# A hybrid attention and expert-lookup layer on one core: the order around the head groups' norms and the way of the gate row

## The chip, the core and the metric

The kernel runs on one core of a Trainium2 chip (trn2). The metric is the device time of one execution in microseconds, lower is better; several runs are given by their median. The engines are named as in the profile: PE (TensorE), PEld (its weight loads), DVE (VectorE), ACT (ScalarE), POOL (GpSimd) and SP (SyncE), which issues the kernel's DMAs in one queue, in order.

## The reference, cut to what matters

One decoder layer for 256 tokens of width 2048, in float32. `c` is a condition vector that makes six rows of scales, shifts and gates.

```python
mod = jnp.dot(jax.nn.silu(c), w_ada) + b_ada
sh1, sc1, g1, sh2, sc2, g2 = split(mod, 6)
h = layer_norm(x) * (1 + sc1) + sh1
proj = jnp.dot(h, w_in)                       # 4160 columns
qa, ka, va, cq, ckv, kr = split(proj)         # va: columns 2048 to 3071
o_a = dilated_mixture(rope(qa), rope(ka), va)           # 8 heads of 128
o_b = mla_attention(... rms_norm(cq), rms_norm(ckv) ...)  # 8 heads of 128
o = concatenate([rms_norm(o_a, g_out_a), rms_norm(o_b, g_out_b)])
mix = jnp.dot(o, w_o)
x = layer_norm(alpha * x + g1 * mix, ln1_g, ln1_b)
h = layer_norm(x) * (1 + sc2) + sh2
x = layer_norm(alpha * x + g2 * peer(h, ...), ln2_g, ln2_b)
```

Both groups' outputs are normed over all 1024 columns of the group (root of the mean square), so a group's norm needs its last head.

## The kernel before, in words

**Layout.** Tokens lie on the 128 partitions in two halves (`th`), features along the free axis. A weight comes from memory in pieces of 512 rows by 512 columns, 1 MB each, loaded by SP into a ring of three `raw` buffers. A product with nearly full float32 precision takes three passes (`mm3`, L139 to 142): ACT casts the piece to `hi` (L101), DVE subtracts for `lo` (L103), two halves to a piece, in rings of four halves each; PE then multiplies hi·hi, hi·lo and lo·hi. Some early pieces are multiplied as plain float32 (L334).

**The condition rows.** `w_ada` has 96 blocks of 1 MB. `ada` (L207 to 213) loads one into a buffer (a ring of two, tag "ada") and DVE multiplies and sums it against the activated condition in two passes (L212). The first 32 blocks are woven into w_in by hand (`ada_in`). The other 48 of sub-layer 1 and 2 come from a generator, `ada_rest` (L246): `ada_pull(n)` draws the next n, first the 16 of the gate row G1, then the second sub-layer's shifts and scales. Where it is called, and with which number, is in the tuples `PULLS`, `PULL_WO` and `PULL_PQ` (L42 on).

**w_in** (L315 to 346): four groups of 512 input rows (kg), eight pieces of 512 columns in each, in two halves of the rows. Sums over the groups are added in `proj` in SBUF by DVE (L346). Group 3 is ordered by the attention: `latents` (L519) takes pieces 6 and 7 (the latents of group B), then 0, 2, 4; then 1, 3 and 5 (L580). Piece 4 has the values of dilated heads 0 to 3, piece 5 those of heads 4 to 7.

**Attention.** Heads run one after another: `attend` (L415) has PE compute scores, DVE add the mask and take the maximum, ACT the exponential, PE three transposes (L438), ACT a copy, PE the product with the values (L442 to 444), ACT the scaled result into `proj` (L446, helper L240). Group A has the dilated heads, group B the latent ones. The order is a0, a1, a2, a3, then b0 to b3, then b4 to b7, each followed by a pull, then the norm of group B, a4 and a5, group B's operands, a6 and a7.

**Norms and operands.** `row_norm` (L458) has ACT square all 1024 columns with a running sum (L462), DVE and ACT make the inverse root (`rstd_of`, L166: a square root on ACT and six small DVE operations), and the rows are scaled in place, one half by DVE (L468), the other by ACT. `to_operand` (L488) then transposes 512 columns at a time on PE (L481), scales them on ACT with the gain (L485), casts (L160) and subtracts (L161) into the operand `act` of w_o.

**w_o** (L239 on): 16 pieces. Steps 0 to 3 use the rows of group B only (column blocks 0 and 1); they are put ahead of the norm of group A in the text (L624). Then `g1b`, the gate row on all partitions, is made by `spread_cols` (L230): for each of 16 columns a diagonal tile on DVE (L235) and a product with ones on PE (L236), four copies on ACT (L237). Steps 4 to 11 follow; at the end of a column block `residual` (L642) multiplies with `g1b`, adds x and takes statistics; the first is at step 7. The layer norm, w_pq and the expert stages follow; they fill three quarters of the span.

**What sets the order.** Each engine runs its instructions in a fixed order, made when the program is built: the text's order is the priority, and an operation that a model of the engines has ready comes ahead of one that waits. `issue_after` puts the instructions of a block behind a given one on its engine.

## Time and profile before

| | |
|---|---|
| median of 3 runs | 2043.37 us (2042.28 to 2044.26) |
| the profiled execution's own time | 2044.22 us |
| its span | 2042.4 us |
| mean granted clock of PE | 0.984 |
| busy share PE, DVE, ACT, POOL | 97%, 73%, 51%, 0% |
| moved by DMA | 554.82 MB |

Times in the trace count from the start of the span. A line of the windows view has the stretch, its length, then for PE, PEld, DVE, ACT and POOL the busy time with the number of instructions in brackets, then the granted clock of PE as a share of full speed (1.00 is 2.4 GHz, 0.50 is 1.2 GHz), the share of the DMA engines' time, and GB/s. A line of the timeline has start, duration, engine, line of the kernel, operation, output and inputs, shapes, count, and in square brackets how long the engine was idle before and what released it. Product durations include the array's depth; from start to start they are shorter.

### The profile page before, as it was taken

To read this page: it belongs to the slowest core of one execution; us is meant where nothing else is said; L and a number is where in the kernel's file an instruction comes from. 1 tells how busy PE (TensorE), PEld (TensorE's weight loads), DVE (VectorE), ACT (ScalarE), POOL (GpSimd) and SP (SyncE) were. 2 spreads that over 40 slices of the span, in tenths; PEclk is the share of its full clock that TensorE was granted. 3 is DMA by queue.
4 is the path that set the end of the run, shared out by engine and by line. 5 is a ranking of instruction groups with operands and counts; after the bars stand their busy time and mean duration, and the time that the engine had idled before them with its cause. 6 is when DMAs were issued, how large, how long until landed. Compare 5 with 4: busy or idle time off the path is not lost.

```text
span 2042.4 us, 26235 instructions
## 1 busy us (share of the span) xinstructions
PE 1973.8 (97%) x10072; PEld 1644.3 (81%) x10072; DVE 1497.3 (73%) x2344; ACT 1048.2 (51%) x1538; POOL 0.2 (0%) x4
## 2 busy tenths in 40 slices
PE   6999998988999999999999999999999999999997
PEld 4567686778998888888888888888888788888886
DVE  7588987889799868677777766686776666554557
ACT  2333457435444665677777775444444444444451
POOL 0000000000000000000000000000000000000000
PEclk7999998998999999999999999999999999999999
DMA  8887887867646566667777668989999988765552
GB/s 349 338 332 304 314 324 268 331 267 277 241 147 215 219 239 254 235 255 273 270 287 265 266 238 308 316 337 324 329 337 324 304 290 286 278 227 202 189 207 102
DMA packets 142830, 554.82 MB, mean 272 GB/s; under 512 B 10864, under 2 KB 77552, under 8 KB 84848
## 3 DMA queue, kind: packets, MB, share of 16 engines
q1 hardware_dynamic: 142704, 553.14, 73.5%
q8 instruction: 79, 1.29, 0.2%
q14 instruction: 47, 0.39, 0.1%
HBM read 502.76 MB, written 50.34 MB: 271 GB/s over the span
## 4 chain that ended last, share of the span: by engine, by line
PE 85%; DVE 9%; DMA 3%; ACT 2%; issue 1%; SPq 0%; DVEq 0%; ACTq 0%
PE u_ps L135 21%; PE u_ps L136 11%; PE v_ps L141 10%; PE v_ps L140 10%; PE v_ps L142 10%; PE win_ps L334 3%; DVE ada L212 2%; PE win_ps L141 2%; DMA gl<-g_d 2%; PE win_ps L142 2%; PE g_ps L942 2%; PE win_ps L140 1%; PE wo_ps L142 1%; PE wo_ps L141 1%; PE wo_ps L140 1%
## 5 line engine op out<-in xcount | busy, mean ns | idle before, releaser
L135 PE MATMUL u_ps<-act,hi_u 128*128 128x512 f32 x2048 | 721.6, 396 | 0.0
L136 PE MATMUL u_ps<-act,lo_u 128*128 128x256 f32 x2048 | 575.1, 281 | 0.9 <-DVE lo_u L103 0.9
L135 PEld LDWEIGHTS u_ps<-act,hi_u 128*128 128x128 f32 x2048 | 384.5, 188 | 87.7
L101 ACT CAST hi_v<-raw_v 128x1024 fp32r<-128x1024 f32 x244 | 256.8, 1054 | 332.0 <-PE v_ps L142 298.6
L103 DVE TENSOR_TENSOR lo_v<-raw_v,hi_v 128x1024 fp32r<-128x1024 f32 x244 | 295.6, 1222 | 173.0 <-ACT hi_v L101 172.9
L103 DVE TENSOR_TENSOR lo_u<-raw_u,hi_u 128x1024 fp32r<-128x1024 f32 x256 | 312.3, 1221 | 137.7 <-ACT hi_u L101 136.5
L136 PEld LDWEIGHTS u_ps<-act,lo_u 128*128 128x128 f32 x2048 | 386.6, 189 | 3.9 <-DVE lo_u L103 3.7
L141 PE MATMUL v_ps<-lo_v,whi 128*128 128x512 f32 x976 | 380.0, 389 | 2.3 <-DVE lo_v L103 2.3
L140 PE MATMUL v_ps<-hi_v,whi 128*128 128x512 f32 x976 | 379.9, 389 | 1.0 <-DVE W L798 1.0
L142 PE MATMUL v_ps<-hi_v,wlo 128*128 128x512 f32 x976 | 379.7, 389 | 0.0
L101 ACT CAST hi_u<-raw_u 128x1024 fp32r<-128x1024 f32 x256 | 267.3, 1048 | 174.4 <-PE u_ps L135 163.3
L141 PEld LDWEIGHTS v_ps<-lo_v,whi 128*128 128x128 f32 x976 | 183.2, 188 | 41.0 <-DVE lo_v L103 3.5
L140 PEld LDWEIGHTS v_ps<-hi_v,whi 128*128 128x128 f32 x976 | 183.2, 188 | 40.1 <-DVE W L798 1.8
L142 PEld LDWEIGHTS v_ps<-hi_v,wlo 128*128 128x128 f32 x976 | 183.2, 188 | 38.1
L212 DVE SCALAR_TENSOR_TENSOR ada<-ada,cb 128x1024 f32<-128x1024 f32 x160 | 191.0, 1218 | 9.9 <-DMA ada<-in_w_ada_dram 9.8
L937 DVE TENSOR_TENSOR o<-eq,gT 128x1024 fp32r<-128x1024 f32 x64 | 78.3, 1223 | 33.3 <-PE g_ps L942 33.3
L334 PE MATMUL win_ps<-raw_win,hmod 128*128 128x512 f32 x192 | 86.4, 605 | 1.2 <-ACT hmod L305 1.2
L799 ACT ACTIVATE W<-W 128x512 f32<-128x512 f32 x64 | 40.7, 636 | 73.4 <-DVE W L798 73.4
L140 PE MATMUL wpq_ps<-act,hi_wpq 128*128 128x256 f32 x256 | 73.6, 290 | 2.3 <-ACT act L160 2.1
L142 PE MATMUL wpq_ps<-act,lo_wpq 128*128 128x256 f32 x256 | 72.8, 286 | 0.5 <-DVE lo_wpq L103 0.5
L141 PE MATMUL wpq_ps<-act,hi_wpq 128*128 128x256 f32 x256 | 73.0, 286 | 0.0
L101 ACT CAST hi_win<-raw_win 128x1024 fp32r<-128x1024 f32 x40 | 40.9, 1049 | 61.4 <-PE win_ps L142 30.8
(329 smaller groups left out, 2407.1 us busy)
## 6 DMA issues: line engine op xcount, KB each, us to landing
raw_u<-in_u_dram SPq DMA_DIRECT2D x128, 1024.0 KB, 5.3
raw_v<-in_v_dram SPq DMA_DIRECT2D x122, 1024.0 KB, 6.6
ada<-in_w_ada_dram SPq DMA_DIRECT2D x80, 1024.0 KB, 6.9
raw_win<-in_w_in_dram SPq DMA_DIRECT2D x32, 1024.0 KB, 8.9
g_d<-stg SPq DMA_DIRECT2D x16, 2048.0 KB, 7.2
gl<-g_d SPq DMA_DIRECT2D x32, 1024.0 KB, 10.1
raw_wo<-in_w_o_dram SPq DMA_DIRECT2D x16, 1024.0 KB, 6.9
raw_wpq<-in_w_pq_dram SPq DMA_DIRECT2D x16, 1024.0 KB, 6.9
```

The costliest lines, as they stand in the source:

```text
L101: nc.scalar.copy(hi, raw[:, 2 * j:2 * j + 2, :])
L103: nc.vector.tensor_sub(lo, raw[:, 2 * j:2 * j + 2, :], hi.bitcast(F32))
L135: nc.tensor.matmul(pss[e], hi[:, i, es], act[:, k], start=first and j == 0 and i == 0, stop=False)
L136: nc.tensor.matmul(pss[e][:, 1], lo[:, i, es], act_hi[:, k, :], start=False, stop=last and j == 1 and i == 3)
L140: nc.tensor.matmul(o, sh, mh, start=start, stop=False)
L141: nc.tensor.matmul(o, sh, ml, start=False, stop=False)
L142: nc.tensor.matmul(o, sl, mh, start=False, stop=stop)
L212: nc.vector.scalar_tensor_tensor(w[:, z, :], w[:, z, :], 1.0, cb[:, z * 1024:(z + 1) * 1024], op0=ALU.mult, op1=ALU.mult, accum_out=(modc, ...
L334: nc.tensor.matmul(ps[th], act[:, i, ts], src[:, i, :], start=i == 0, stop=i == 3)
L799: nc.scalar.activation(ws, ws, AF.Gelu)
L937: nc.vector.tensor_mul(o2, eq.unsqueeze(2).broadcast_to(both), gT[:, four, :].bitcast(F32).unsqueeze(3).broadcast_to(both))
L942: nc.tensor.matmul(ps[:, q * T:(q + 1) * T], o1[:, 2 * j + q, :], o2[:, 2 * j + q].rearrange("p z n -> p (z n)"), start=True, stop=True)
```

## The change

- Piece 5 of w_in's group 3 (the values of a4 to a7) leaves its place between the latents and a0. It is loaded and split ahead of head b7, and its products are issued behind b7's last product, in front of the norm of group B. The scores of a4 and a5 come in front of it.
- Each group's squares are split: those of the first seven heads are taken early (`early_squares`), only the last head's at the end. The inverse root takes fewer DVE operations.
- The norm and the operands of group A come ahead of w_o's steps 0 to 3 in the text. The pulls of these steps are put behind that norm on DVE.
- The gate row is transposed as soon as its sixteen blocks are there, written to memory (`row_d`), and read back to all partitions by one DMA, in place of the spread.
- Pulls move: six into w_in's group 1 (one behind each of the six sets of pieces), none any more with piece 5 or behind b4 to b6 and b7, and other numbers in w_o.

```diff
-PULLS = (2, 1, 1, 3, 0, 1, 1, 1, 3, 1, 0, 1)
-PULL_WO = (2, 3, 0, 1, 1, 1, 1, 1, 0, 0, 1, 2)
+PULL_IN = (0, 1, 0)
+PULLS = (2, 1, 1, 3, 0, 1, 1, 1, 3, 1, 0, 0)
+PULL_WO = (0, 1, 1, 1, 1, 1, 1, 1, 1, 1, 1, 2)
...
     def rstd_of(pool, var, n, eps):
         uid[0] += 1
         ve = pool.tile([P, n], F32, tag=f"rs_ve{n}", name=f"rs_ve{uid[0]}", bufs=1)
         nc.vector.tensor_scalar(ve, var, eps, None, op0=ALU.add)
+        return rstd_from(pool, ve, n)
+
+    def rstd_from(pool, ve, n):
         r = pool.tile([P, n], F32, tag=f"rs_r{n}", name=f"rs_r{uid[0]}", bufs=4)
         nc.scalar.activation(r, ve, AF.Sqrt)
         nc.vector.reciprocal(r, r)
         t = pool.tile([P, n], F32, tag=f"rs_t{n}", name=f"rs_t{uid[0]}", bufs=1)
         nc.vector.tensor_mul(t, r, r)
-        nc.vector.tensor_mul(t, t, ve)
-        nc.vector.tensor_scalar(t, t, -0.5, 1.5, op0=ALU.mult, op1=ALU.add)
-        last_rstd[0] = nc.vector.tensor_mul(r, r, t)
+        nc.vector.scalar_tensor_tensor(t, t, -0.5, ve, op0=ALU.mult, op1=ALU.mult)
+        last_rstd[0] = nc.vector.scalar_tensor_tensor(r, t, 1.5, r, op0=ALU.add, op1=ALU.mult)
         return r
...
-    def spread_row(pool, col0, dst):
-        ps = bank("sm", "spread")
+    def row_of(col0):
+
+        ps = bank("tr", f"row_ps{col0}")
         nc.tensor.transpose(ps[:16, :P], modc[:, col0:col0 + 16], ident)
-        rowt = pool.tile([16, P], F32, name="rowt")
+        rowt = stream.tile([P, 2, 512], F32, tag="lo", name=f"rowt{col0}", bufs=4)[:16, 0, :P]
         nc.scalar.copy(rowt, ps[:16, :P])
         nc.sync.dma_start(row_d.rearrange("(c p) -> c p", p=P), rowt)
-        bcast_row(dst, row_d)
...
             ada_bias(G1, 16)
+            row_of(G1)
...
                         ada_in(kg + 1, m)
                         m += 1
+                    ada_pull(PULL_IN[kg])
...
-            def row_norm(c0, n, name):
-
-                ms = mix.tile([P, 2], F32, tag="ms", name=f"ms_{name}", bufs=2)
+            def squares(c0, n, ms):
                 for th in range(2):
                     nc.scalar.activation(junk[:, :n], proj[:, th, c0:c0 + n], AF.Square, accum_out=ms[:, th:th + 1])
-                nc.vector.tensor_scalar(ms, ms, 1.0 / n, None, op0=ALU.mult)
-                r = rstd_of(mix, ms, 2, 1e-6)
+
+            def row_norm(c0, n, name, early=None):
+
+
+                ms = mix.tile([P, 2], F32, tag="ms", name=f"ms_{name}", bufs=2)
+                if early is None:
+                    squares(c0, n, ms)
+                    nc.vector.tensor_scalar(ms, ms, 1.0 / n, 1e-6, op0=ALU.mult, op1=ALU.add)
+                else:
+                    squares(c0 + n - P, P, ms)
+                    nc.vector.scalar_tensor_tensor(ms, ms, 1.0 / n, early, op0=ALU.mult, op1=ALU.add)
+                uid[0] += 1
+                r = rstd_from(mix, ms, 2)
                 done = last_rstd[0]
...
+            def early_squares(c0, name):
+                ms = mix.tile([P, 2], F32, tag="mse", name=f"mse_{name}", bufs=1)
+                squares(c0, 1024 - P, ms)
+                nc.vector.tensor_scalar(ms, ms, 1.0 / 1024, 1e-6, op0=ALU.mult, op1=ALU.add)
+                return ms
...
-            for n in (1, 3, 5):
+            for n in (1, 3):
                 w_in_pieces(3, (n,), hmod3)
                 ada_pull(PULLS[2])
...
-            for h in (4, 5, 6, 7):
+            for h in (4, 5, 6):
                 heads_b(h)
                 ada_pull(PULLS[11])
-            row_norm(1024, 1024, "ob")
-            heads_a(2, last_a[0])
+            ms_b = early_squares(1024, "ob")
+            first[3, 5] = piece(a["w_in"][3, 5], "win3_5")
+            heads_b(7)
+
+            last_s = [scores_a(*last_a[0], h) for h in (4, 5)]
+            with tc.issue_after(last_o[0].ins):
+                w_in_pieces(3, (5,), hmod3)
+            row_norm(1024, 1024, "ob", ms_b)
+            heads_a(2, last_a[0], scores=last_s)
             to_operand(1024, 8, V_GOUT + 8, "ob0")
             to_operand(1536, 12, V_GOUT + 12, "ob1")
-            heads_a(3, last_a[1])
+            heads_a(3, last_a[1], (0,))
+            ms_a = early_squares(0, "oa")
+            heads_a(3, last_a[1], (1,))
+            norm_done = row_norm(0, 1024, "oa", ms_a)
+            to_operand(0, 0, V_GOUT, "oa0")
+            to_operand(512, 4, V_GOUT + 4, "oa1")
             for step in range(4):
                 w_o_piece(step)
-            norm_done = row_norm(0, 1024, "oa")
-            to_operand(0, 0, V_GOUT, "oa0")
-            to_operand(512, 4, V_GOUT + 4, "oa1")
...
-            spread_cols(g1b, modc[:, G1:G1 + KC], "g1")
+            bcast_row(g1b, row_d)
...
                 if step >= 4:
                     w_o_piece(step)
-                ada_pull(PULL_WO[step])
+                    ada_pull(PULL_WO[step])
+                else:
+                    with tc.issue_after(norm_done.ins):
+                        ada_pull(PULL_WO[step])
```

`attend` now gets its scores in a bank that its caller has filled (`scores_a` for group A), and it keeps its last product in `last_o`.

## Rows read from the trace of the kernel before

**Rows 1.** The page, part 1: busy time, share of the span and instructions of each engine.
```profile
PE 1973.8 (97%) x10072; PEld 1644.3 (81%) x10072; DVE 1497.3 (73%) x2344; ACT 1048.2 (51%) x1538; POOL 0.2 (0%) x4
```
**Rows 2.** The windows view, by stages of w_in and of the attention's end and w_o.
```profile
92.50:113.40 20.90, 20.90 (x51) 9.42 (x51) 12.64 (x21) 1.99 (x2) 0.00 (x0) 1.00 0.72 294
113.40:142.50 29.10, 27.42 (x120) 22.04 (x120) 28.39 (x47) 9.93 (x11) 0.00 (x0) 1.00 0.98 398
142.50:163.70 21.20, 21.20 (x74) 12.41 (x73) 14.29 (x23) 4.79 (x7) 0.00 (x0) 1.00 0.55 216
163.70:171.00 7.30, 4.35 (x13) 3.15 (x13) 7.30 (x13) 4.52 (x6) 0.00 (x0) 0.77 1.00 423
332.80:348.10 15.30, 9.21 (x39) 6.83 (x37) 11.50 (x53) 13.65 (x29) 0.00 (x0) 0.67 0.67 253
348.10:372.40 24.30, 24.25 (x114) 19.67 (x115) 21.92 (x47) 17.44 (x28) 0.00 (x0) 1.00 0.73 280
372.40:386.80 14.40, 9.78 (x55) 7.68 (x53) 12.44 (x29) 8.52 (x15) 0.00 (x0) 0.88 0.71 258
386.80:451.40 64.60, 64.60 (x283) 53.20 (x284) 55.55 (x78) 23.74 (x24) 0.00 (x0) 1.00 0.80 319
```
**Rows 3.** The waits from 325 to 390 us: who waited, for whom, total, times, longest.
```profile
PE pt_a L438 <- DVE mx_a L433: 4.9, 4, 3.6
```
**Rows 4.** The timeline around the norm of group B and the first w_o product.
```profile
333.75 1.05 ACT L462 ACTIVATE qr_lt<-proj 128x1024 f32<-128x1024 f32 x1
...
336.78 1.28 ACT L171 ACT_TABLE_LOAD   x1
...
338.07 0.20 ACT L171 ACTIVATE rs_r<-rs_ve 128x2 f32<-128x2 f32 x1
...
341.55 1.15 ACT L240 ACTIVATE proj<-proj,rs_r 128x1024 f32<-128x1024 f32 x1
...
348.06 0.19 PEld L140 LDWEIGHTS wo_ps<-hi_wo,act 128*128 128x128 f32 x1 [0.51 <-ACT act L160]
```
**Rows 5.** ACT's groups by shape, 332.8 to 386.8 us: count, busy, mean ns, idle before.
```profile
L485 ACT ACTIVATE qr_lt<-ob_ps,cols 128x256 f32<-128x256 f32 x8 | 3.3, 474 | 1.2 <-PE ob_ps L481 0.9 <-DVE act L161 0.3
...
L240 ACT ACTIVATE proj<-o_a,mx_a 128x128 f32<-128x128 f32 x8 | 2.5, 364 | 0.6 <-PE o_a L444 0.4
L237 ACT COPY g1b<-g_ps 128x512 f32<-128x512 f32 x4 | 2.3, 586 | 4.0 <-PE g_ps L236 2.1 <-PE wo_ps L140 1.9
...
L431 ACT ACTIVATE e_a<-sm_a,mx_a 128x256 f32<-128x256 f32 x4 | 2.0, 502 | 0.0
L440 ACT COPY pt_a<-pt_a 128x384 f32<-128x384 f32 x4 | 1.9, 476 | 0.0
L431 ACT ACTIVATE e_a<-sm_a,mx_a 128x128 f32<-128x128 f32 x4 | 1.6, 395 | 0.0
```
**Rows 6.** DMA issues, 1100 to 1800 us: KB each, median us from issue to landing.
```profile
cb<-row_d SPq DMA_DIRECT2D x1, 1024.0 KB, 12.6
```
**Rows 7.** DVE's groups by shape in the second w_in group, 113.4 to 142.5 us.
```profile
L212 DVE SCALAR_TENSOR_TENSOR ada<-ada,cb 128x1024 f32<-128x1024 f32 x9 | 10.7, 1219 | 0.0
```
**Rows 8.** DMA issues, 95 to 180 us.
```profile
raw_win<-in_w_in_dram SPq DMA_DIRECT2D x15, 1024.0 KB, 7.5
ada<-in_w_ada_dram SPq DMA_DIRECT2D x13, 1024.0 KB, 10.8
```
**Rows 9.** The timeline of DVE at the start of the second w_in group.
```profile
96.28 1.22 DVE L212 SCALAR_TENSOR_TENSOR ada<-ada,cb 128x1024 f32<-128x1024 f32 x1
```
**Rows 10.** The timeline of PE in w_in: two waits, and the last piece's first products.
```profile
115.42 0.50 PE L141 MATMUL win_ps<-lo_win,act 128*128 128x512 f32 x1 [1.58 <-DVE lo_win L103]
...
136.84 0.61 PE L140 MATMUL win_ps<-hi_win,act 128*128 128x512 f32 x2
...
167.30 0.79 PE L141 MATMUL win_ps<-lo_win,act 128*128 128x512 f32 x1 [2.95 <-DVE lo_win L103]
```

More of the change, by code (lines that the diff above doesn't have):

```diff
@@ L413, in rope, with attend @@
                 nc.vector.tensor_add(x2, tmp[0], tmp[2])
-            def attend(qk_mm, scale, neg, cnt, v, o_cols, name):
-                ps = bank("mm", f"s_{name}")
-                qk_mm(ps)
+            def attend(ps, scale, neg, cnt, v, o_cols, name):
                 sm = t384("sm", f"sm_{name}")
@@ L443, in attend @@
                 nc.tensor.matmul(pso[:, 128:256], pt[:, 128:256], v(0), start=True, stop=False)
-                nc.tensor.matmul(pso[:, 128:256], pt[:, 256:384], v(1), start=False, stop=True)
+                last_o[0] = nc.tensor.matmul(pso[:, 128:256], pt[:, 256:384], v(1), start=False, stop=True)
                 for th in range(2):
@@ L544, in heads_a_in, with scores_a, heads_a @@
                 return head_t(hp * 256, f"q{hp}", "qT"), head_t(1024 + hp * 256, f"k{hp}", "kT")
-            def heads_a(hp, qkT=None):
+            def scores_a(qT, kT, h):
+                i = h % 2
+                ps = bank("mm", f"s_a{h}")
+                nc.tensor.matmul(ps[:, 0:128], qT[:, i, 0:128], kT[:, i, 0:128], start=True, stop=True)
+                nc.tensor.matmul(ps[:, 128:384], qT[:, i, 128:256], kT[:, i, :], start=True, stop=True)
+                return ps
+            def heads_a(hp, qkT=None, heads=(0, 1), scores=None):
                 qT, kT = qkT or heads_a_in(hp)
-                for i in range(2):
+                for i in heads:
                     h = 2 * hp + i
-                    def qk(ps):
-                        nc.tensor.matmul(ps[:, 0:128], qT[:, i, 0:128], kT[:, i, 0:128], start=True, stop=True)
-                        nc.tensor.matmul(ps[:, 128:384], qT[:, i, 128:256], kT[:, i, :], start=True, stop=True)
-                    attend(qk, 128.0 ** -0.5, cc(C_NEGA, 384), cc(C_CNT, 384),
+                    ps = scores[i] if scores else scores_a(qT, kT, h)
+                    attend(ps, 128.0 ** -0.5, cc(C_NEGA, 384), cc(C_CNT, 384),
                            lambda kb: proj[:, kb, 2048 + h * P:2048 + (h + 1) * P],
```

5 lines of the change are left out of this document (4 added, 1 removed).

## The prediction, before the run

> **What bounds the kernel now.** I read the page first: TensorE is busy for 97% of the span [rows 1], so time can be won only where it waits or runs at its lower clock. The windows by stage [rows 2] show two such places close together. From the last product of the B heads (332.8) to the first w_o product (348.1) PE is busy for 9.21 of 15.3 us at a mean granted clock of 0.67, while ACT is busy for 13.65. From 372.4 to 386.8, behind w_o's steps 0 to 3, PE is busy for 9.78 of 14.4 us at 0.88, and part of that is the gate row's spread. Between them (348.1 to 372.4) and behind them (386.8 to 451.4) PE is full at clock 1.00. The waits [rows 3] name the first hole: PE waits 4.9 us for the softmax of a dilated head. The timeline [rows 4] has what stands behind it: the squares of group B start at 333.75, the table for the square root loads at 336.78, the rows are scaled at 341.55 and the first w_o product starts at 348.06, at which ACT is the releaser. The last stage to look at is the second group of w_in (113.4 to 142.5 in rows 2), because the change puts new work there: DVE is busy for 28.39 of 29.1 us and the DMA share is 0.98. PE, DVE and the transfers are all full in that stage.
>
> **The change part by part.** Sums are made against the profiled execution's own 2044.22 us (2042.4 of span and 1.8 around it). The median of the runs shown is 2043.37, 0.85 lower, and I take that off at the end.
>
> *Value columns held back.* The piece is 24 products; the second w_in group, all of such products, does 120 in 27.42 us [rows 2], 0.229 each: 5.5 us of PE, which leave a stage where PE is full and go into the first hole. Its two lo passes, two additions and its pull of w_ada leave with it, so DVE does not hold the shortened stage up. I take -5.5; bounds 0 (DVE is the limit there anyway) and -5.5. In its new place its time is inside the next term.
>
> *The two holes.* From 332.8 to 386.8 are 54.0 us [rows 2]. I rebuild them from the last B product on. ACT has, up to the first w_o product: two scale-outs of the last B head (0.6), two squares over 128 columns, the table load and square root (1.5) and the load back (1.28), half the rows' scaling (1.15), and for heads a4 and a5 exponentials 1.8, copies 0.95, scale-outs 1.25, then four scalings (1.65) and a cast as wide as the 1,024-wide square (1.05) for the first operand [rows 4, 5]. A 128-wide square has no row: below it stands a 128-wide scale-out (0.31), above it the 1,024-wide square (1.05); I take 0.5 each, since the narrow rows are nearest. Sum 12.2 us. PE meanwhile has 5.5 us of held-back products and the work of a4 and a5, so it waits some 3 us there instead of 6, and at the higher clock for longer. Then PE has the 24.3 us of the full stage [rows 2] and the 16 transposes of group A, 2.8 us as their share of the 55 instructions and 9.78 busy us of the second hole: 12.2 + 24.3 + 2.8 = 39.3. ACT in that second part has what it had from 348.1 to 386.8, 17.44 + 8.52, less the spread's four copies (2.3, rows 5), plus about 0.9 for the split squares: 24.5, against PE's 27.1. They are close, so I add 3.7 us of waits that neither hides and get 43. Term: -11.0; bounds 39.3 us (-14.7) and 50 us (-4, rival 2). The gate row's 16 diagonal tiles and 32 products go with the second hole. If the operand of group A is late all the same, step 4 of w_o waits for it, since its first product of that group stands there.
>
> *Gate row through DRAM.* One PE transpose and a small copy early, and two DMAs. The nearest row for the broadcast is the later one of the same kind, 1 MB landing in 12.6 us [rows 6]. It is first read at the end of step 7, and steps 4 to 7, 96 products, are 22 us of cover; the DMA share from 386.8 to 451.4 is 0.80 [rows 2]. I take 0. Without that cover DVE's first residual, and the two PSUM banks behind it, would wait the 12.6 us. The early write waits on SP for the copy, and what SP has queued behind it waits too: 0 to 1 us, taken as 0.
>
> *Pulls of w_ada.* Six move into the second w_in group, one behind each piece; four leave the last B heads, one goes with the held-back piece, and w_o gets one fewer in all but two more in steps 4 to 11. Each pull is a 1 MB transfer, at 423 GB/s [rows 2] 2.5 us, and two DVE passes of 1.22 [rows 7], 2.45 us. In 386.8 to 451.4 DVE goes from 55.6 to 60.5 of 64.6 us: still behind PE, 0. The three pulls of steps 0 to 3 now stand behind group A's root on DVE, the next transfer waits for their buffers, and w_o's loads stand behind it on SP; the share there is 0.73, so I take 0, at most one transfer's 2.5. In 113.4 to 142.5 nothing is left: five pulls come ahead of the group's end, one finds DVE's idle time before it (12.64 of 20.9 us busy), and four cost 2.45 each. DVE's lo pass of the next piece stands behind the pull, and PE and the PSUM additions wait for that. The later stages do not give it back, since PE is full there and moves with it. Term: +9.8; bounds +2.5 (rival 1) and +22.6 (rival 3).
> For the transfers the row shows 423 GB/s from 163.7 to 171 and 398 over the 29.1 us. The Trainium skill (DMA: Bandwidth & Descriptors, section Where 436 GB/s comes from) says that for loads from HBM the memory's share of about 358 GB/s binds; by that rule a pull would take 2.93 us, an estimate from the page, four would cost 11.7, and the time would be 2038. The trace is above that rate, so the row decides.
>
> *Small operations of the norms.* Each inverse root loses one DVE pass and group norms lose two; at about 0.2 us of chain for each exposed layer norm I take -0.6; bounds 0 and -1.5.
> For the square root's table the rows show a load of 1.28 us and the root 1.29 us after its start [rows 4]. The Trainium skill (ScalarE: Activation LUTs, section What ACT_TABLE_LOAD costs) puts a switch at 2.66 us with a drain and tells the author to do all of one set before the other; by that rule the two switches ahead of the first w_o product would add 2.8 us, an estimate from the page, and the time would be 2039. The trace shows no such drain.
>
> Sum: 2044.2 - 5.5 - 11.0 - 0.6 + 9.8 = 2036.9; less 0.85, **2036.1 us**.
>
> **The rivals.**
> 1. *The early pulls ride in idle time.* For: the transfers' share is 0.72 from 92.5 to 113.4 and 0.55 from 142.5 to 163.7, and DVE has 15 idle us in the two [rows 2]. Against: the buffers that would have to be free are two, and the order of each engine is fixed when the program is built. One pull's price is left: 2044.2 - 17.1 + 2.5 - 0.85 = 2028.8.
> 2. *ACT takes the hole's place.* ACT is busy for 13.65 of the first hole's 15.3 us, and the change takes little from it there: it adds split squares, and casts of w_o pieces that lost their place to the held-back piece's. If the chain of group A's norm then ends behind step 3, the 54 us become 50: 2044.2 - 5.5 - 4 - 0.6 + 9.8 - 0.85 = 2043.1. This is also the case in which the planned order puts the transposes behind the w_o products in spite of their earlier place in the text.
> 3. *Slower: the two-slot ring of w_ada holds SP up.* The extra pulls use the ring of two buffers, and w_in's loads stand behind them on SP. From issue to landing a w_ada transfer takes 10.8 us here [rows 8], and the broadcast of 1 MB later on took 12.6 [rows 6]; with 2.45 on DVE, and up to as much for another pull's passes ahead of it, a slot turns in 13.3 to 17.5 us. Each slot serves three users before pull 5; from 97.5, when DVE is through with the first tile of this stage [rows 9], pull 5 is then issued at 137 to 150, and the last piece's load, behind it, lands 7.5 later [rows 8], with some 2 us of casts to come. PE would start that piece at 147 to 159 instead of 136.8 [rows 10], 10 to 22.6 late. It decides from a turn of about 15.7 us on, where the loss passes the 17.1 us gained: 2044.2 - 17.1 + 22.6 - 0.85 = 2048.9. A clock that falls belongs to such stalls: with a wait of 1.58 us the second group keeps clock 1.00, around one of 2.95 the mean is 0.77 [rows 2, 10].
>
> **How the numbers follow.** A measurement tells 0.2%, 4.1 us, from no change. Forecast 0.48, with its own range 2031 to 2041 (0.40 faster, 0.08 the same); rival 1 0.20 (faster); rival 2 0.18 (0.14 the same, 0.03 faster, 0.01 slower); rival 3 0.14 (0.12 slower, 0.02 the same). Faster 0.63, same 0.24, slower 0.13. The range runs from a little under rival 1 to short of rival 3, 2027.5 to 2046.5, and leaves about 0.17 out.
>
> **What would show it.** Right: the w_in products of the held-back piece directly behind the last B product; no wait of PE over 3 us and clock 1.00 in the stretch that answers to 332.8 to 386.8, now near 43 us; no spread products; group A's transposes among the products of steps 0 to 3. The second w_in group some 39 us long, with PE waiting for DVE's lo passes. Rival 1: that group near 31 us. Rival 2: the transposes of group A behind step 3 with ACT as releaser. Rival 3: SP waiting on w_ada's buffers for most of the group and ACT's casts waiting for w_in's loads. I am wrong if the change in the two stages does not add up to the change of the whole.

## The result and the profile after

The changed kernel takes 2063.65 us (median of 4 runs, 2062.20 to 2065.20) against 2043.82 us (4 runs, 2042.28 to 2047.03): a ratio of 1.0093, 95% interval 1.0077 to 1.0109. It is 20 us slower, outside the forecast's range on the slow side. The profiled execution took 2062.2 us, with a span of 2060.3.

The page's first part shows where not to look. It answers to [rows 1]: every engine did the work it did before.

```profile
PE 1975.7 (96%) x10040; PEld 1642.5 (80%) x10041; DVE 1494.2 (73%) x2314; ACT 1045.7 (51%) x1543; POOL 0.2 (0%) x4
```

So the 20 us are waits. The windows view of the kernel after, by the stages of [rows 2] (PE, PEld, DVE, ACT and POOL busy, then granted clock, DMA share, GB/s):

```profile
91.30:112.10 20.80, 20.80 (x51) 9.32 (x51) 12.54 (x21) 1.99 (x2) 0.00 (x0) 1.00 0.70 283
112.10:161.40 49.30, 36.02 (x123) 26.47 (x122) 40.96 (x68) 11.71 (x15) 0.00 (x0) 0.86 0.87 357
161.40:182.60 21.20, 21.20 (x73) 12.28 (x72) 15.21 (x26) 3.02 (x4) 0.00 (x0) 1.00 0.52 206
347.90:362.60 14.70, 11.47 (x67) 9.12 (x65) 9.95 (x44) 14.64 (x33) 0.00 (x0) 1.00 0.03 5
362.60:372.40 9.80, 9.80 (x44) 7.85 (x45) 4.13 (x12) 8.27 (x20) 0.00 (x0) 0.83 0.26 102
372.40:386.80 14.40, 14.24 (x71) 11.42 (x70) 12.45 (x20) 11.00 (x19) 0.00 (x0) 1.00 0.48 185
386.80:471.00 84.20, 76.20 (x311) 59.72 (x311) 70.24 (x106) 27.74 (x31) 0.00 (x0) 0.94 0.87 355
```

Two things stand out. The second w_in group's split pieces, 29.1 us in [rows 2], are now 49.3 us, at a DMA share that fell from 0.98 to 0.87. And from 347.9 to 386.8 the queue is nearly idle (0.03, 0.26, 0.48), while the w_o products after it have PE busy for 76.20 of 84.20 us, where they had 64.60 of 64.60.

A ledger of the two profiled executions, from starts and ends of products in the timeline (us):

| stretch | before | after | difference |
|---|---|---|---|
| to the second w_in group's first product | 92.6 | 91.3 | -1.3 |
| that group, to the third group's first long row of products | 50.9 | 71.6 | +20.7 |
| from there to the last B product | 189.4 | 184.7 | -4.7 |
| last B product to first w_o product | 15.2 | 15.0 | -0.2 |
| first to last w_o product | 103.3 | 108.0 | +4.7 |
| to the first w_pq product | 20.6 | 21.5 | +0.9 |
| the rest | 1570.4 | 1568.2 | -2.2 |

The prediction wanted some 9.8 us more in the second row, and 11 us less in the fourth and fifth rows together.

**The second w_in group.** The timeline of DVE in the kernel after shows one turn per piece:

```profile
122.20 2.35 DVE L104 TENSOR_TENSOR lo_win<-raw_win,hi_win 128x1024 fp32r<-128x1024 f32 x2
124.47 1.22 DVE L216 SCALAR_TENSOR_TENSOR ada<-ada,cb 128x1024 f32<-128x1024 f32 x1
...
125.62 1.22 DVE L216 SCALAR_TENSOR_TENSOR ada<-ada,cb 128x1024 f32<-128x1024 f32 x1
...
129.04 0.69 DVE L351 TENSOR_TENSOR proj<-proj,win_ps 128x512 f32<-128x512 f32 x1 [2.20 <-PE win_ps L143]
129.65 1.22 DVE L216 SCALAR_TENSOR_TENSOR ada<-ada,cb 128x1024 f32<-128x1024 f32 x1
...
130.79 0.68 DVE L351 TENSOR_TENSOR proj<-proj,win_ps 128x512 f32<-128x512 f32 x1
131.39 1.22 DVE L216 SCALAR_TENSOR_TENSOR ada<-ada,cb 128x1024 f32<-128x1024 f32 x1
...
132.53 2.35 DVE L104 TENSOR_TENSOR lo_win<-raw_win,hi_win 128x1024 fp32r<-128x1024 f32 x2
```

And the timeline of PE in the same group:

```profile
123.48 0.50 PE L142 MATMUL win_ps<-lo_win,act 128*128 128x512 f32 x1 [1.98 <-DVE lo_win L104]
...
133.81 0.50 PE L142 MATMUL win_ps<-lo_win,act 128*128 128x512 f32 x1 [1.60 <-DVE lo_win L104]
...
144.13 0.54 PE L142 MATMUL win_ps<-lo_win,act 128*128 128x512 f32 x1 [2.16 <-DVE lo_win L104]
...
154.46 0.62 PE L142 MATMUL win_ps<-lo_win,act 128*128 128x512 f32 x1 [2.98 <-DVE lo_win L104]
```

It is a closed loop. DVE idles for 2.20 us until PE has finished the piece, then does two additions with two w_ada passes between and behind them, and only then the next piece's lo pass, for which PE waits. The turns are 10.3 us (123.48, 133.81, 144.13, 154.46) for a piece with 5.5 us of products. Both engines wait in every turn, because the next lo pass stands *behind* the additions of the present piece. Two more w_ada passes follow each lo pass, in time that DVE would else spend waiting. The group's whole DVE work has grown too: over the second row of the ledger DVE is busy for 55.03 us, 41.64 before.

**The end of attention.** The timeline of SP in the kernel after:

```profile
336.27 0.33 SPq L86 DMA_DIRECT2D raw_wo<-in_w_o_dram  x1
...
361.33 20.30 SPq L86 DMA_DIRECT2D raw_wo<-in_w_o_dram  x3
382.44 2.62 SPq L214 DMA_DIRECT2D ada<-in_w_ada_dram  x2
```

Between 337 and 382 SP asks for three transfers in all; in the kernel before it asked for eleven of w_ada and w_o between 340 and 382. The hold itself is on DVE. Between 325.7 and 378.2 us DVE makes no pass over w_ada, and the first one comes right behind the last step of group A's root:

```profile
378.17 0.16 DVE L181 SCALAR_TENSOR_TENSOR rs_r<-rs_t,rs_r 128x2 f32<-128x2 f32 x1
378.25 1.22 DVE L216 SCALAR_TENSOR_TENSOR ada<-ada,cb 128x1024 f32<-128x1024 f32 x1
```

Until then the transfers issued at 320.11 and 329.70 occupy both buffers of w_ada, and no further one can start. The waits of ACT from 400 to 472 us in the kernel after say what the lost time costs later:

```profile
ACT hi_wo L102 <- DMA raw_wo<-in_w_o_dram: 26.1, 5, 9.2
```

### The profile page after: what moved, and what is told of

It is laid out like the page before. It is cut to its first block, busy times and chain, and to the rows that moved or that the text cites. A ratio compares the mean times of both kernels' runs of the same rounds, so it can differ in the third digit from the quotient of the medians.

```text
span 2060.3 us, 26138 instructions
## 1 busy us (share of the span) xinstructions
PE 1975.7 (96%) x10040; PEld 1642.5 (80%) x10041; DVE 1494.2 (73%) x2314; ACT 1045.7 (51%) x1543; POOL 0.2 (0%) x4
## 4 chain that ended last, share of the span: by engine, by line
PE 86%; DVE 7%; DMA 3%; ACT 2%; issue 1%; SPq 0%; DVEq 0%; ACTq 0%
PE u_ps L136 22%; PE u_ps L137 11%; PE v_ps L142 10%; PE v_ps L143 10%; PE v_ps L141 10%; PE win_ps L339 3%; DVE ada L216 2%; PE win_ps L142 2%; DMA gl<-g_d 2%; PE win_ps L143 2%; PE g_ps L978 1%; PE win_ps L141 1%; PE wo_ps L142 1%; PE wo_ps L143 1%; PE wo_ps L141 1%
## 5 line engine op out<-in xcount | busy, mean ns | idle before, releaser
L137 PEld LDWEIGHTS u_ps<-act,lo_u 128*128 128x128 f32 x2048 | 386.8, 189 | 2.9 <-DVE lo_u L104 2.7
L216 DVE SCALAR_TENSOR_TENSOR ada<-ada,cb 128x1024 f32<-128x1024 f32 x160 | 190.0, 1218 | 10.6 <-DMA ada<-in_w_ada_dram 10.4
L142 PE MATMUL win_ps<-lo_win,act 128*128 128x512 f32 x160 | 67.1, 419 | 15.8 <-DVE lo_win L104 15.5
L141 PE MATMUL wpq_ps<-act,hi_wpq 128*128 128x256 f32 x256 | 73.3, 289 | 2.0 <-ACT act L161 1.8
```

The costliest lines, as they stand in the source:

```text
L137: nc.tensor.matmul(pss[e][:, 1], lo[:, i, es], act_hi[:, k, :], start=False, stop=last and j == 1 and i == 3)
L141: nc.tensor.matmul(o, sh, mh, start=start, stop=False)
L142: nc.tensor.matmul(o, sh, ml, start=False, stop=False)
L216: nc.vector.scalar_tensor_tensor(w[:, z, :], w[:, z, :], 1.0, cb[:, z * 1024:(z + 1) * 1024], op0=ALU.mult, op1=ALU.mult, accum_out=(modc, ...
```

## The experiments

Theory A: the six early pulls stretch the second w_in group. Theory B: the hold of the pulls of steps 0 to 3 (`issue_after(norm_done)`) leaves the queue idle and makes the w_o steps short of transfers. Repeated runs of one kernel scatter by 2 to 12 us, so medians are compared, and differences under about 2 us are not read. The kernel before was timed again beside the runs, which are compared with its medians of 2044.24, 2044.90, 2045.35 and 2044.35.

### Putting the two suspects back

`e1_pulls_back`, on the kernel after:
```diff
-PULL_IN = (0, 1, 0)
+PULL_IN = (0, 0, 0)
-PULLS = (2, 1, 1, 3, 0, 1, 1, 1, 3, 1, 0, 0)
+PULLS = (2, 1, 1, 3, 0, 1, 1, 1, 3, 1, 0, 1)
-PULL_WO = (0, 1, 1, 1, 1, 1, 1, 1, 1, 1, 1, 2)
+PULL_WO = (0, 1, 1, 1, 1, 1, 1, 1, 1, 1, 2, 2)
                 ada_pull(PULLS[2])
+            ada_pull(PULLS[2])
             heads_a(0)
...
             heads_b(7)
+            ada_pull(PULLS[11])
```


> The kernel after, with the six early transfers of w_ada put back: none in the second w_in group, five of them behind the old site of piece (3,5) and behind heads b4 to b7, one in the w_o steps; the three of steps 0 to 3 still wait for group A's root. Theory A (the six pulls stretch the second w_in group from about 50 to 69 us, because the vector engine's passes over them stand between one piece's adds and the next piece's residual casts): the group is about 50 us again, its 10.3 us pieces are 5.4 us, and the time falls by 16 to 19 us to 2045 to 2048. Theory B alone (the loss comes from the hold and the late loads in the w_o steps): the time moves by less than 5 us, above 2058. Rival (the held-back piece and the early norm on the scalar engine cost the time): above 2058 too, with the first w_o product still about 362.

`e2_no_hold`, on the kernel after:
```diff
-                    with tc.issue_after(norm_done.ins):
-                        ada_pull(PULL_WO[step])
+                    ada_pull(PULL_WO[step])
```


> The kernel after, with the transfers of w_ada of steps 0 to 3 free to start when their buffers are (three transfers), the six early ones left where they are. Theory B (these held transfers leave the queue idle from 340 to 380 us and make the w_o steps short of transfers): three transfers of about 2.5 us each move into the idle time, DMA share in 340 to 380 rises from about 0.16 to 0.3, and the w_o steps get 5 to 8 us shorter: 2056 to 2059. Theory A alone: within 2 us of 2063.7, since the second w_in group is untouched. Rival (the hold protects the norms' vector work, as it is meant to): slower by 2 to 5 us, with the second norm's chain later.

`e3_both` has both edits.


> The kernel after with both edits: the six transfers back in their old places and none held behind group A's root. If A and B are both right and add up: 2045 to 2048 less 3 to 8, so 2038 to 2044, faster than or level with the kernel before. If B is worth nothing once five transfers run in 300 to 345 us: the same as with the transfers put back alone, 2045 to 2048. If the held-back piece and the reordered norms themselves lose: above 2048.

`e4_before_pulls_early`, on the kernel before: `PULL_IN`, its call, `PULLS[11]` and piece 5's pull as in the kernel after, and `PULL_WO[0]` 1 for 2.


> The kernel before with nothing but the six transfers moved into the second w_in group, one after each of its six steps. Theory A: the group is stretched by 15 to 19 us as in the kernel after, and since the later stretches are not short of transfers the whole comes to 2055 to 2062. Rival (the six transfers ride in the group and the stall in the kernel after comes from elsewhere in the change): 2042 to 2048. What I put on them in the prediction, 9.8 us: 2053.

| kernel | median us (runs) | ratio to before, 95% | second group | last B to first w_o | w_o products |
|---|---|---|---|---|---|
| before | 2043.82 (4) | | 50.9 | 15.2 | 103.3 |
| after | 2063.65 (4) | 1.0077 to 1.0109 | 71.6 | 15.0 | 108.0 |
| e1 pulls back | 2043.14 (10) | 0.9979 to 0.9999 | 51.0 | 15.0 | 106.4 |
| e2 no hold | 2047.87 (10) | 1.0008 to 1.0034 | 69.7 | 15.0 | 93.2 |
| e3 both | 2036.14 (4) | 0.9933 to 0.9971 | 51.0 | 15.2 | 100.1 |
| e4 pulls alone | 2066.01 (4) | 1.0085 to 1.0131 | 71.6 | 16.5 | 104.2 |

Both theories hold, and all four effects are larger than I expected: e1, e2 and e3 lie below their ranges and e4 above its own. The early pulls alone, on the kernel before, cost 21.8 us, and taking them back out of the kernel after gains 20.5; the stall belongs to them and to nothing else in the change. The hold costs 15.8 us with the pulls early (2063.65 to 2047.87) and 7.0 with them in their old places (2043.14 to 2036.14). The two do not simply add: without the hold, taking the early pulls back gains only 11.7 (2047.87 to 2036.14), because the group gets shorter but the w_o steps get longer (100.1 us against 93.2). The trace of e2 is of its fastest run, 2042.61, so its stages may be a little short. I had expected 5 to 8 for three held transfers. The timeline of SP in e2 shows what else was held:

```profile
337.13 5.68 SPq L214 DMA_DIRECT2D ada<-in_w_ada_dram  x2
...
349.44 4.62 SPq L214 DMA_DIRECT2D ada<-in_w_ada_dram  x2
362.04 0.33 SPq L86 DMA_DIRECT2D raw_wo<-in_w_o_dram  x1
364.37 8.93 SPq L214 DMA_DIRECT2D ada<-in_w_ada_dram  x3
...
378.08 0.33 SPq L214 DMA_DIRECT2D ada<-in_w_ada_dram  x1
```

Eight w_ada transfers start where the kernel after has none until 382.44. The pulls keep their order and share two buffers, so passes held for three of them keep the buffers full and move every later pull behind group A's root too. The loads of w_o were not held: the next one comes at 361.33 in the kernel after and at 362.04 in e2. In e2 the w_o steps then run as the prediction had them; the windows view from its first to its last w_o product:

```profile
364.30:457.90 93.60, 93.46 (x421) 74.98 (x422) 78.31 (x126) 47.41 (x67) 0.00 (x0) 1.00 0.79 314
```

### What the early pulls do to the group

`e5_casts_ahead`, on e2: the next piece is loaded and split before the present piece's last additions, and these are ordered behind its lo pass, in the second group alone.
```diff
+                if ahead is not None:
+                    first[kg, ahead] = piece(a["w_in"][kg, ahead], ...)
                 for n, ps in zip(ns, pss):
...
+                            with tc.issue_after(last_lo[0].ins):
+                                nc.vector.tensor_add(dst, dst, ps[th])
```


> The run e2 (change without the hold, six transfers still in the second w_in group), with one thing more: in that group the next piece's two residual passes are put ahead of the present piece's adds on the vector engine, so that no piece waits for the vector passes over w_ada of the piece before. The group was 51.0 us before, 69.7 in e2, with 55.1 us of vector work and, at its DMA share of 0.84, 58.5 us of transfers. Theory A1 (the order of the passes makes a loop tensor engine, adds and w_ada passes, residual pass, tensor engine of 10.3 us a piece): the loop is gone and the group falls to what the transfers need, 58 to 62 us; the time falls from 2047.9 to 2037 to 2042. Theory A2 (the two w_ada buffers that the queue waits for hold up the w_in loads behind them, whatever the vector order): the group stays at 66 us or more, with the scalar engine's casts waiting for raw_win, and the time within 4 us of 2047.9.

`e6_loads_only`, on e2 (with `modc` and `modh` cleared first):
```diff
-        for z in range(2):
+        for z in range(0 if G1 <= j < G1 + 6 else 2):
```


> The run e2 with the six early transfers of w_ada still loaded in the second w_in group but without their vector passes (two per transfer, 14.6 us in all); the gate's first six columns then keep only their bias. If the vector passes make the stretch (A1): the group falls from 69.7 to 55 us or less. If the transfers make it (six of about 2.45 us on a queue that was 0.87 busy: 44.3 + 14.7 = 59 us): 58 to 62 us. If the two buffers make it (A2): they come free as soon as the next load may start, so this falls too, and it is told from A1 by e5. What I put on the transfers in the prediction, 9.8 us, would be 61 us.

`e12_passes_only`, on e2:
```diff
-        nc.sync.dma_start(w, a["w_ada"][j]...)
+        if not early:
+            nc.sync.dma_start(w, a["w_ada"][j]...)
...
+            ... cb[:, z * 1024:(z + 1) * 1024] if early else w[:, z, :] ...
```


> The run e2 with the six early transfers of w_ada not loaded, while their vector passes are kept (they read the activation row in place of the weights, so the gate's first six columns are another number). The counterpart of e6, in which the loads alone made the second w_in group 62.3 us, 11.4 more than 50.9, of the 18.8 more in e2. If loads and passes add up: 50.9 + 7.4 = 58 us. If the loop of passes is what sets it whenever they are there: 64 us or more. If the passes hide once the loads are gone: 53 us or less.

The windows view of the whole second group, from its first product to the third group's, in e2:

```profile
90.59:160.26 69.67, 56.00 (x186) 35.73 (x186) 55.14 (x91) 15.09 (x18) 0.00 (x0) 0.93 0.84 340
```
The same view in e5:
```profile
92.52:158.11 65.59, 53.45 (x182) 34.13 (x182) 55.27 (x92) 13.22 (x16) 0.00 (x0) 0.94 0.85 340
```
In e6:
```profile
88.88:151.16 62.28, 53.01 (x186) 33.76 (x186) 43.65 (x69) 13.31 (x16) 0.00 (x0) 0.97 0.87 357
```
In e12:
```profile
91.05:159.72 68.67, 55.94 (x174) 35.05 (x174) 55.91 (x91) 13.40 (x15) 0.00 (x0) 0.93 0.72 285
```

The group is 50.9 us without early pulls, 69.7 with them, 68.7 with their passes alone and 62.3 with their loads alone. (e6 and e12 leave out work and were run once: 2035.22 and 2043.50 us, beside 2042.61 for the traced run of e2.) So the two do not add up (17.8 and 11.4 against 18.8): they run side by side, and the later one ends the stage. The passes are the later one. e12 is the run that decides: six fewer loads, the DMA share down at 0.72, SP waiting ahead of w_ada's loads for 24.0 us from 95 to 160 (14.1 of them behind DVE's passes) instead of e2's 39.0 (36.3), and still nearly the same length. What PE waits for in the group (from 91 to 160 us) is the same too, first in e2 and then in e12:

```profile
PE win_ps L142 <- DVE lo_win L104: 9.3, 5, 3.0
```
```profile
PE win_ps L142 <- DVE lo_win L104: 8.8, 5, 3.1
```

In e12 PE never waits for ACT's hi casts, so w_in's loads were in time. A1 expected e6 at 55 or less; it is 62.3, so the loads set a second floor. Part of it is transfer time: the queue worked 0.87 x 62.28 = 54.2 us in e6, and 20.9 x 0.72 + 29.1 x 0.98 = 43.6 before [rows 2], 10.6 less. The rest is what the ring of two would do; the waits of SP in e6 from 95 to 160 us have it waiting for w_ada's transfers to land before it may issue the next:

```profile
SPq L217 <- DMA ada<-in_w_ada_dram: 21.6, 5, 7.3
```

Breaking the loop in e5 gained 4.1 us of group and 3.4 us of time (2044.51, 10 runs, ratio 0.9985 to 1.0005). That is less than A1 expected (2037 to 2042), and at the edge of what A2 expected (a group of 66 us or more, it is 65.6, and a time within 4 us of 2047.9); taken alone, e5 would not have told the two apart. The loop did go: PE's waits for lo passes fall from 9.3 us in e2 to 2.7. But DVE then has no time left over the split pieces. The windows view of e5 there:

```profile
113.30:152.30 39.00, 30.64 (x121) 22.96 (x119) 38.56 (x58) 9.71 (x11) 0.00 (x0) 0.96 0.89 359
```

So the larger part of the cost is not the order but the work. All twelve early passes run in the group (28 passes over w_ada in e2 and e5, 16 before), and none of them in DVE's idle time at its start: the first 21 us have eight of these passes in e2 and eight before. The group of e5 is 14.7 us longer than before, about the price of six pulls at 2.45. The order adds 4.1 to that. This split is read from the trace of e5; passes alone, with the loop broken, were not run. In e5 the loads are not far behind either: in its waits from 92 to 160 us PE waits 3.8 us for ACT's hi casts, and these 37.1 us for raw_win, 19.1 of them at the group's start; another 5.6 us PE waits at the group's end for the next group's modulated rows (3.2) and for a small load (2.4). How the floor of the loads divides between the queue's rate and the two buffers stays open; a third buffer was not tried.

### Is there a free place for the pulls

`e7_first_sets`, on e3: `PULL_IN = (0, 2, 2)` behind the first set of each group alone, `PULL_WO = (0, 0, 1, 1, 1, 1, 0, 1, 1, 1, 1, 1)`.


> The run e3 (change without the hold and with the six transfers back, 2036.1), with four transfers taken out of the w_o steps and put beside the first sets of the second and third w_in groups, two each, where the tensor engine works for 20 us on products that need no casts and the vector engine stood idle. If only the place in the group mattered (the passes between adds and casts of the later pieces): the groups grow by at most 4 us together, the w_o steps, 100.1 us in e3 and short of transfers, fall towards the 93.2 of e2, and the time is 2030 to 2035. If the queue in these groups is what fills (DMA share 0.87 and 0.80): the groups grow by the four transfers' 9.8 us and the time is 2036 to 2042.

`e10_pulls_sooner`, on e9 (below): `PULL_WO = (2, 2, 1, 1, 1, 1, 1, 1, 1, 1, 1, 0)`.


> The run e9 with the transfers of w_ada of the w_o steps asked for sooner (two each in steps 0 and 1, none in the last; 13 in all as before). In e3 the queue is busy for 0.45, 0.49 and 0.68 of 330 to 360 us and the w_o steps are short of transfers after 400 us (100.1 us against 93.2 with four to six transfers fewer). If the order of the requests decides: two or three more transfers fall into 330 to 360, the w_o steps take 94 to 97 us and the time is 2029 to 2033. Rival (the two buffers and the vector engine's passes, 0.89 to 0.97 busy in 340 to 360, hold them back anyway): the w_o steps stay at 99 to 101 and the time is that of e9; and if the passes push group A's root back: slower than e9 by 1 to 3 us.

`e13_end_of_first_group`, on e3: two pulls behind the first group's last piece, `PULL_WO` ending in 1, 1.


> The run e3 with two transfers of w_ada taken out of the last w_o steps and put behind the last piece of the first w_in group, where the queue is 0.49 busy (80 to 92 us) and the vector engine 0.66. Price of the place: they ride free there, the w_o steps fall by 3 to 5 us, and the time is 2031 to 2034. Price of the transfer: the first or second group grows by what the w_o steps lose, and the time is 2035 to 2038.

`e14_three_later`, on e3: `PULL_WO` ending in 1, 0 and `PULL_PQ[2]` 3.


> The run e3 with three transfers of w_ada moved from the last two w_o steps to the third piece of w_pq, which is ahead of where their columns are first read. Price of the place: the w_o steps fall from 100.1 us towards 94, the w_pq stage (101.9 us, the tensor engine full, DMA share 0.81 to 0.96 in its first half and below 0.55 in its second) keeps its length, and the time is 2030 to 2033. Price of the transfer: the w_pq stage grows by 5 to 7 us and the time is 2035 to 2038.

`e15_both_places`, on e9: the two pulls of e13, `PULL_WO` ending in 0, 0 and `PULL_PQ[2]` 2.


> The run e9 with two transfers at the end of the first w_in group as in e13, two moved to the third piece of w_pq, and so four fewer in the w_o steps. If the price is one of the place: the w_o steps near 93 us and the time 2028 to 2032. If each transfer costs its 2.5 us in whichever full stage it stands: 2035 to 2039, no better than e3 and e9.

| kernel | median us (runs) | ratio to before, 95% | where the pulls went | w_o products |
|---|---|---|---|---|
| e3 | 2036.14 (4) | 0.9933 to 0.9971 | | 100.1 |
| e7 | 2040.08 (10) | 0.9968 to 0.9987 | second group 51.0 to 57.8 | 93.3 |
| e10 | 2037.23 (7) | 0.9951 to 0.9978 | | 102.6 |
| e13 | 2038.80 (10) | 0.9963 to 0.9985 | second group 51.0 to 54.1 | 100.3 |
| e14 | 2041.83 (10) | 0.9980 to 1.0002 | w_pq products 101.9 to 111.0 | 98.0 |
| e15 | 2034.96 (8) | 0.9951 to 0.9973 | 54.2, and w_pq 108.8 | 94.7 |

None of these places is free, as the second reading in each expectation had it. In e7 the w_o steps lose 6.8 us, but the second group gains 6.8 and the stretch from there to the last B product 5.4. In e15 they lose 5.1 against e9, and the second group gains 3.2 and w_pq 6.9. In e14 w_pq gains 9.1 for 2.1 lost, and the time is above both readings. In e13 the second group grows and the w_o steps lose nothing. In e10 nothing is won, which was the rival: the calls stand earlier in the text, but the next three w_ada transfers start from 347.67 on, 1.1 us behind the first w_o product, and those of e9 from 342.84 on, 1.1 behind as well. In e14 a new wait appears; in its waits from 467 to 578 us PE waits for ACT's operand, whose columns of w_ada are late:

```profile
PE wpq_ps L141 <- ACT act L161: 6.8, 2, 5.0
```

e3, e9 (2035.68) and e15 can't be told apart. All three beat both kernels, by 0.4 to 0.5% of the kernel before.

### The other parts

`e8_piece_back`, on e3: piece (3,5) computed beside 1 and 3.


> The run e3 with the last value columns' piece (3,5) computed in its old place beside pieces 1 and 3, so that what is left of the change is the norms' order, the split squares, the shorter root and the gate row through DRAM. My prediction gave the held-back piece 5.5 us: 2041.6 by that. If it fills a hole of 15 us that is no shorter for it, it is worth its own 5.4 us of products and less what comes later: 2039 to 2042, with the first w_o product still 15 us behind the last product of the B heads. Rival (its cast buffers hold back the w_o loads, so that it costs as much as it gives): 2034 to 2037.

`e9_adds_after_root`, on e3, where `w_in_pieces` of (3,5) hands back its two additions as `add_values`:
```diff
-            row_norm(1024, 1024, "ob", ms_b)
+            b_done = row_norm(1024, 1024, "ob", ms_b)
+            with tc.issue_after(b_done.ins):
+                add_values()
```


> The run e3 with one change: the vector engine's two adds of the held-back piece (3,5) stand behind the last step of group B's root instead of ahead of it. In e3 the first of these adds waits 1.62 us for the piece's products while the root's last step is queued behind it (334.18 to 336.57), and the hole from the last product of the B heads to the first w_o product is 15.2 us; with the piece in its old place (e8) it is 13.5. Theory: the in-order wait on the vector engine is what keeps the hole as long as before; the hole falls to 13 to 13.5 us and the time to 2033.5 to 2035. Rival (the scalar engine's queue of head A's work and casts sets the hole): the hole stays at 15 and the time at 2036.

`e11_gate_spread`, on e3:
```diff
-            bcast_row(g1b, row_d)
+            spread_cols(g1b, modc[:, G1:G1 + KC], "g1")
```


> The run e3 with the gate row built as in the kernel before (sixteen diagonals on the vector engine, products with ones, four copies) in the place of the row through DRAM. My prediction gave the gate row 0: 2036 within 1.5 us. Rival (one broadcast load of 1 MB on a queue that is short in the w_o steps costs about 2.5 us, against work on engines that have room): faster, 2033 to 2035. The other rival (the sixteen diagonals and copies sit in the vector queue in front of the w_o steps' passes): slower, 2038 to 2041.

e8 takes 2038.16 us (6 runs, ratio 0.9958 to 0.9983): the held-back piece is worth 2.0, not 5.5, and 2.0 is at the edge of what the scatter lets one read. The stretch ahead of the last B product is 192.7 against 187.9, so 4.8 us did leave; but the hole is 13.5 us without the piece and 15.2 with it. Why, was my next question. The timeline of DVE in e3 has the piece's first addition ahead of the root's last step:

```profile
334.18 0.16 DVE L180 SCALAR_TENSOR_TENSOR rs_t<-rs_t,ms_ob 128x2 f32<-128x2 f32 x1
335.96 0.69 DVE L351 TENSOR_TENSOR proj<-proj,win_ps 128x512 f32<-128x512 f32 x1 [1.62 <-PE win_ps L143]
336.57 0.15 DVE L181 SCALAR_TENSOR_TENSOR rs_r<-rs_t,rs_r 128x2 f32<-128x2 f32 x1
```

In e9 the root is ready at once (331.06, 0.20 behind the step before it), and nothing is gained: 2035.68 us (6 runs, ratio 0.9943 to 0.9973), hole 15.2. That theory fell. My rival, ACT's queue, is not what the rows show either. In e9 the timeline of PE has the first transposes of group B here:

```profile
333.64 0.39 PE L143 MATMUL win_ps<-hi_win,act 128*128 128x512 f32 x1
333.88 0.49 PE L444 MATMUL pt_a<-ident,e_a 128*128 128x128 f32 x3
...
335.69 0.38 PE L448 MATMUL o_a<-proj,pt_a 128*128 128x128 f32 x2
...
336.57 0.60 PE L502 MATMUL ob_ps<-ident,proj 128*128 128x128 f32 x4
```

From 333.64 to 337.18 PE works without a gap, and ACT's half of the scaled rows is done at 333.20 and DVE's at 334.06; the transposes wait for PE's own queue, in which the held-back products and head a4 stand first. That reading was not tested by moving the transposes up, and there is another. The held-back piece's products run at the lower clock at first in e3 and not in e11 (below), which has the same piece in the same place. The windows view of these products, in e3 and then in e11:

```profile
329.96:337.13 7.17, 7.17 (x27) 5.75 (x27) 3.98 (x22) 5.43 (x13) 0.00 (x0) 0.76 0.62 227
```
```profile
329.60:335.15 5.55, 5.55 (x27) 4.54 (x26) 4.39 (x23) 5.37 (x15) 0.00 (x0) 1.00 1.00 412
```

They take 1.6 us less in e11, and its hole is 13.5 us, as short as that of e8 without the piece. So the 1.7 us that e8 seems to show may be the clock's and not the piece's. Nor is the clock all: in the kernel after it is 1.00 there, ACT is busy for 15.08 of 15.14 us (347.46 to 362.60), and the hole is 15.0. What sets the hole's length stays open.

e11 takes 2043.18 us (10 runs, 2040.12 to 2051.64, ratio 0.9982 to 1.0009): 7 us above e3 by medians, 3.1 by the two profiled spans (2038.6 and 2035.5). The timeline of PE in e11 shows what came back:

```profile
370.80 1.31 PE L240 MATMUL g_ps<-g_dg,ones 128*128 128x128 f32 x10
...
372.90 0.94 PE L240 MATMUL g_ps<-g_dg,ones 128*128 128x128 f32 x6 [0.32 <-DVE g_dg L239]
...
375.10 1.16 PE L240 MATMUL g_ps<-g_dg,ones 128*128 128x128 f32 x8 [0.80 <-ACT g1b L241]
...
376.65 1.13 PE L240 MATMUL g_ps<-g_dg,ones 128*128 128x128 f32 x8 [0.39 <-DVE g_dg L239]
...
378.43 0.50 PE L142 MATMUL wo_ps<-lo_wo,act 128*128 128x512 f32 x1 [0.65 <-DVE lo_wo L104]
```

In these 7.6 us the engine that bounds the stage makes a row, does four products of w_o and waits for 2.2 us; the w_o steps are 103.1 us, against 100.1 in e3. With the row through DRAM, e3 pays one wait of DVE, 1.7 us, for a broadcast that landed in 10.3 [rows 6: 12.6].

## Why the prediction was wrong, step by step

- **Two steps failed, both on pulls of w_ada.** The first is "Term: +9.8", four pulls at 2.45 each. They cost 20.7 us of group in the profile, 18.8 without the hold, 21.8 of time alone. The price of one pull by DVE's work was about right and the count was wrong: "one finds DVE's idle time before it" and "five pulls come ahead of the group's end" left four, but all six ran inside the full part of the group, and with the loop broken the group is 14.7 us longer (e5), six times 2.45. The rest is the order, 4.1 us: "DVE's lo pass of the next piece stands behind the pull, and PE and the PSUM additions wait for that" was the right sentence, but I took it for one delay, not for a loop that PE and DVE go round for each piece, in which DVE waits too. The 9.8 is near what the loads added to the queue's work in e6 (10.6), which is not what ended the stage.
- The second is "so I take 0, at most one transfer's 2.5" for the held pulls of steps 0 to 3. They cost 15.8 us (7.0 with the pulls back). I had the chain right (the passes wait for the root, "the next transfer waits for their buffers") and priced one transfer; every later pull waited for the same two buffers, eight transfers up to 382 us by e2. The idle 337 to 382 us was a stage in which the kernel before asked for eleven transfers.
- With both: 2036.1 + (20.7 - 9.8) + 15.8 = 2062.8, against 2063.65 measured. That e3, without early pulls and without the hold, takes the forecast's 2036.1 is chance: the forecast without its 9.8 for pulls is 2026.3, so the rest of the change, with the pulls in their old places, gave 8.1 us (2044.24 to 2036.14) where the prediction had 17.1.
- *The two holes, -11.0: near once the hold is gone, as long as the pulls are early.* From the last B product to the last w_o product are 118.5 us before and 108.2 in e2, -10.3; in e3, where the six transfers run in their old places, they are 115.3, -3.2. Of the 54 us, what closed was the second hole, with group A's transposes (385.47 to 389.0 in e2) among the w_o products. The first stayed at 15 us, filled by the held-back piece and not shortened; why is open.
- *Value columns, -5.5:* 4.8 us left the full stage, as the step said; the hole is 1.7 us longer with the piece than in e8, which may be the clock's. Net 2.0 by medians.
- *Gate row, 0:* right for the transfer. Its products, which I let "go with the second hole", come back in e11 and make the w_o steps 3.0 us longer than in e3. *Small operations, -0.6:* not tested by itself.
- *Rival 1* (pulls ride free) fell in e4, e7, e13 and e14. *Rival 2* (group A's chain ends behind step 3) fell: its transposes stand among the w_o products, and the second hole is closed. That the first hole stays long was its part, and in the kernel after ACT is full there, as it said; in e3 it is not (13.14 of 15.44 us from 329.68 to 345.12), and the hole is as long. *Rival 3* had the sign, the place and nearly the size (22.6 us), but the ring of two is not the mechanism that ended the stage: with six loads fewer (e12) the group kept its length, and PE did not wait for ACT's casts. Its 0.14 was too little, chiefly since [rows 2] showed DVE, PE and the queue all full in that very stage.
- *Signs.* PE waiting for lo passes was named and came, in a group of 49.3 us instead of 39. "No wait of PE over 3 us" held (the longest from 347.5 to 402 us is 1.13); "clock 1.00" held but for 362.6 to 372.4, at 0.83. The loss of the second stage came behind this stretch, where the w_o steps were short of loads. That the two stages should add up to the whole was the right test, and it led straight to the two causes.

## What to carry to other kernels

Work added to an engine that is full in a stage lengthens the stage by all of it: count every pass, and take none off for idle time that the order does not reach (14.7 of 18.8 us here). Then look at the turn of the loop that the pass joins, which instruction stands behind it and who waits for that (4.1 us here); the place to look is the order of the next piece's cast against this piece's additions. Passes held back keep their buffers, and a small ring then stops every later transfer into it, so count the transfers that ran in that stretch before. A transfer moved out of a full stage is only won where neither the queue, nor the engine that consumes it, nor its reader is the limit; here five runs tried other places and none was free.

## What was not expected of the hardware

PE's clock fell in the stall of every turn but the first. In the kernel after, 144.10 to 151.50 us, behind a wait of 2.16 us that followed one of 0.55, the windows view has a granted clock of 0.77, and the timeline shows products at 0.43 us from start to start (1.2 GHz) for 3.4 us and at 0.23 (2.4 GHz) after that:

```profile
144.47 0.63 PE L143 MATMUL win_ps<-hi_win,act 128*128 128x512 f32 x1
144.90 0.63 PE L141 MATMUL win_ps<-hi_win,act 128*128 128x512 f32 x1
...
147.88 0.39 PE L143 MATMUL win_ps<-hi_win,act 128*128 128x512 f32 x1
148.11 0.39 PE L141 MATMUL win_ps<-hi_win,act 128*128 128x512 f32 x1
```

In that turn eight products took 3.4 us in place of 1.8. The prediction had read from [rows 2, 10] that a wait of 1.58 us keeps the clock at 1.00 and one of 2.95 lowers it. Here the wait of 1.60 us before 133.81, with one of 1.10 and 0.7 us of products ahead of it, lowered it as well (granted 0.77 from 133.80 to 141.20): the longest wait alone does not tell. In e11 a wait of 1.55 us before 328.90, behind waits of 0.44, 0.16 and 0.57, kept the clock at 1.00 (324.00 to 329.50); in e3 one of 1.31 before 328.66, behind 1.10, 0.16 and 0.57, came with 0.73 in the same stretch. The other surprise is how little a part of a cost tells: removing the loads of the early pulls gained 1.0 us of group, removing their passes 7.4, and all of the 18.8 went only with both.
